# Moving four gate units and two modulation units of a streaming encoder step behind the last attention quarter and the last RWKV pair

## The chip, the cores and the metric

The kernel runs on one core of one Trainium2 chip. The metric is the device time of one execution in microseconds (us). Its engines, as the profile names them: PE (TensorE, the matmuls) with PEld (its weight loads), DVE (VectorE), ACT (ScalarE), POOL (GpSimd) and SP (SyncE, which issues nearly all DMAs). Each engine runs its own instructions in the order in which they stand in the program and waits for the others by semaphores, so the order of the rows on an engine decides what can cover a wait.

## What is computed

One layer of a hybrid encoder for 256 prompt tokens (one sequence) and 8 x 16 sample tokens, 384 tokens in all, d = 1024, in float32. The reference, cut to what matters here:

```python
mod = silu(c) @ w_ada + b_ada            # 6 rows of 1024 per sequence: shift1, scale1, gate1, shift2, scale2, gate2
h = rmsnorm(x) * (1 + scale1) + shift1
P = h @ w_in                             # columns: RWKV-7 | attention and indexer | two branch gates
o_a = rwkv7(P_rw, ...)                   # 16 heads of 64
o_b = dsa(P_dsa, ...)                    # 16 heads of 64, top-k keys by an indexer
gate_a, gate_b = split(sigmoid(P_gate + b_gate))
m = gate_a * (o_a @ w_proj_a) + gate_b * (o_b @ w_proj_b)
x = x + gate1 * (m @ w_out)
h2 = rmsnorm(x) * (1 + scale2) + shift2
x = x + gate2 * peer(h2)                 # 8 heads, 16 of 16384 experts each
```

## The kernel before

The kernel has a front (everything up to the two branch outputs), a mix (gates, projections, `w_out`) and the PEER part. The front ends at about 722 us of a span of 1794 us; the change touches the front alone.

**Units of the front.** After the head (norm, the first eight modulation units, the hidden state `LT` as a high and a low float32r part), a string `ORDER` says in which order the rest is written down, one letter a unit:

- `R`, `rwkv_pair`: two RWKV heads. Three projections of 128 columns (`shifted`), then a long chain of small steps: decay, in-chunk matrices, a triangular inverse that goes through DRAM and 15 steps on VectorE, the state chain, a group norm (`y`), and the store of the result (line 665) to `oad`. Eight pairs, 0 to 7.
- `D`, `dsa_quarter`: four attention heads. Projections K, Q, V of 256 columns each, norm and rotary, sample attention in four rounds (`attend_s`), prompt attention in two blocks (`attend_p`, which ends in `ob` and `qr`), and the store to `obd`. Four quarters, 0 to 3.
- `G`, `gate_unit`: 128 gate columns for all tokens: one weight load of 512 KB, its split into a high part (`wh`, ScalarE, line 230) and a low part (`wl`, VectorE, line 234), 24 matmuls against `LTh` and `LTl`, a sigmoid (`gg`, lines 433 and 434) and a store (line 1153). Sixteen units; nothing reads them before the mix.
- `M`, `mod_unit`: 256 columns of the modulation: two weight loads of 512 KB, eight matmuls of 32 rows against `cst` straight from the loaded weights, a copy (`mr`, line 391) and a store (line 399). Units 8 to 23 stand in `ORDER`; nothing reads them before the end of the mix.
- `I` is the indexer with its own pools, `1` to `3` choose the keys.

So G and M are fillers: they depend on the head alone and have until the mix, while R and D are chains of dependent steps.

**What sets the order.** The letters set the order in which the instructions are written down; a scheduler then places them engine by engine, earlier-written ones first where it thinks them ready. Projections of all kinds share two PSUM buffers (`mm`) and come out on PE in the order of the letters; the small steps of the pairs (`cp`, `bx`, `fx`) and quarters (`dx`) go between them.

**Weights.** All weight loads share one ring of four buffers `w` of 512 KB, four for `wh` and three for `wl` (`WB = (4, 4, 3)`). A G takes one `w` and frees it after its split; an M takes two and frees each when PE has read it. SyncE issues the loads in order.

**The end.** The mix begins with the product of `oad` and `w_proj_a`: it loads `oad` back (`px`, line 1160), splits it (`pbh`, `pbl`) and multiplies (`mm<-pbh,wh`). Its tiles lie where those of the front were.

Of the kernel before, what the change touches and what calls it, by code (L numbers as in the profile page):

```python
# [173 lines left out]

PSB = {"mm": 2, "fx": 2, "bx": 1, "dx": 2, "cp": 1}
ALIAS = {"ix": "cp", "cs": "bx", "u": "fx"}
ORDER = "GGIggggR1R23DMMMGRMRDMRGMGMRMDGMMRRMGDMMMGGGMGGM"


N1, NW, NA, NB = 36, 76, 12, 20  # L180
# [15 lines left out]
class K:  # L196
# [1388 lines left out]
    def run(self):  # L1585
        self.dense = False
        with ExitStack() as front:
# [20 lines left out]
            with ExitStack() as s:  # L1608
# [4 lines left out]
                ds, n = None, dict.fromkeys("RGD", 0) | {"M": 8}  # L1613
                for x in ORDER:
                    if x == "I":
# [130 lines left out]
```

## Time and profile before

| | |
|---|---|
| time, median of 3 runs | 1802.26 us (1799.84 to 1807.32) |
| the profiled execution | 1796.01 us |
| its span, first to last instruction | 1794.1 us |
| mean granted PE clock in it | 0.978 |
| DMA over the span | 434.11 MB, mean 242 GB/s |

A timeline row gives the start, the length, engine, line, operation, tiles (out<-in), shapes and count of merged instructions; in brackets the idle time of the engine ahead of it and what ended it. "PEclk" is the share of full clock that PE was granted. A busy PE is one with a matmul in flight, which says little about how closely they follow each other.

### The profile page before, as it was taken

The numbers are of one execution on the slowest core, as the hardware profiler recorded it, in microseconds if no ns is written. First come the engines' busy times: TensorE is split into PE (matmuls) and PEld (weight loads), VectorE is DVE, ScalarE is ACT, GpSimd is POOL, SyncE is SP. The second block draws the span as 40 slices with busy tenths as digits, with TensorE's granted clock in tenths as the row PEclk, the third lists the DMA queues.
The fourth block names the chain that finished last, engine by engine and source line by source line (L and its number), as shares of the span: only waits on it lengthen the run. The fifth ranks groups of instructions, "written<-read, shape, count | busy, mean of one in ns | idle before, by whom it ended". The sixth has DMA issues, their size and how long they took to land.

```text
span 1794.1 us, 33542 instructions
## 1 busy us (share of the span) xinstructions
PE 1714.5 (96%) x12576; PEld 1420.0 (79%) x12576; DVE 1362.0 (76%) x2945; ACT 703.2 (39%) x1411; POOL 700.5 (39%) x752
## 2 busy tenths in 40 slices
PE   6999899999999999999999989999999999999998
PEld 4987687777878877898888889999967667776656
DVE  3448777777867765445999999899958778887885
ACT  4533343333333333324222264488843333333232
POOL 2432242323423320024054446533356565555641
PEclk7999899999999999999999999999999999999999
DMA  8543652463365364665499989964579999999995
GB/s 298 161 128 96 198 178 63 155 195 97 101 198 158 85 217 151 219 202 166 151 336 333 347 305 370 376 228 164 201 267 373 364 377 379 364 395 345 376 378 182
DMA packets 181082, 434.11 MB, mean 242 GB/s; under 512 B 39348, under 2 KB 78388, under 8 KB 180920
## 3 DMA queue, kind: packets, MB, share of 16 engines
q1 hardware_dynamic: 144056, 297.73, 49.4%
q0 software_dynamic: 36864, 134.23, 20.1%
q8 instruction: 99, 1.62, 0.4%
q14 instruction: 63, 0.52, 0.1%
HBM read 401.65 MB, written 30.24 MB: 241 GB/s over the span
## 4 chain that ended last, share of the span: by engine, by line
PE 67%; DVE 15%; DMA 10%; issue 3%; ACT 2%; POOL 2%; SPq 0%; DVEq 0%; ACTq 0%; POOLq 0%
PE mm L226 24%; PE fx L226 15%; PE dx L226 12%; PE cp L226 8%; PE bx L226 7%; DVE raw L1570 2%; DMA w<-in_pv 2%; DVE wl L234 2%; DVE acc L1580 1%; DMA w<-in_w_ada 1%; DMA raw<-in_pv,pe 1%; DMA w<-in_w_in 1%; DMA w<-in_puT 1%; ACT wh L230 1%; DVE psi L1297 1%
## 5 line engine op out<-in xcount | busy, mean ns | idle before, releaser
L234 DVE TENSOR_TENSOR wl<-w,wh 128x1024 fp32r<-128x1024 f32 (+1 forms) x274 | 343.6, 1259 | 119.6 <-ACT wh L230 58.6
L230 ACT ACTIVATE wh<-w 128x1024 fp32r<-128x1024 f32 (+1 forms) x282 | 295.9, 1054 | 207.5 <-PE mm L226 83.0
L1559 POOL DMA_INDIRECT raw<-in_pu,pe x128 | 154.6, 1208 | 181.1 <-PE dx L226 56.0
L226 PE MATMUL fx<-h2h,wh 128*128 128x256 f32 x736 | 216.1, 294 | 7.5 <-ACT wh L230 4.5
L1559 POOL DMA_INDIRECT raw<-in_pv,pe x128 | 173.0, 1351 | 120.4 <-PE dx L226 44.9
L226 PE MATMUL fx<-h2h,wl 128*128 128x256 f32 x736 | 212.2, 289 | 7.7 <-DVE wl L234 7.4
L226 PE MATMUL fx<-h2l,wh 128*128 128x256 f32 x736 | 209.9, 285 | 0.0
L1580 DVE SCALAR_TENSOR_TENSOR acc<-raw,dots,acc 128x1024 f32<-128x1024 f32 x127 | 165.2, 1301 | 10.3 <-DMA raw<-in_pv,pe 9.1
L1570 DVE SCALAR_TENSOR_TENSOR raw<-raw,sh 128x1024 f32<-128x1024 f32 x128 | 161.8, 1274 | 12.5 <-DMA raw<-in_pu,pe 11.7
L226 PEld LDWEIGHTS fx<-h2h,wh 128*128 128x128 f32 x736 | 140.9, 191 | 12.3 <-ACT wh L230 5.9
L226 PEld LDWEIGHTS fx<-h2h,wl 128*128 128x128 f32 x736 | 140.2, 191 | 10.7 <-DVE wl L234 10.1
L226 PEld LDWEIGHTS fx<-h2l,wh 128*128 128x128 f32 x736 | 141.2, 192 | 2.2 <-issue 1.7
L226 PE MATMUL fx<-h2f,w 128*128 128x256 f32 x576 | 129.9, 387 | 6.0 <-ACT G L1471 3.1
L226 PEld LDWEIGHTS fx<-h2f,w 128*128 128x128 f32 x576 | 111.0, 194 | 23.2 <-ACT G L1471 4.0
L226 PE MATMUL mm<-LTh,wh 128*128 128x384 f32 (+2 forms) x352 | 125.1, 356 | 3.3 <-ACT wh L230 2.7
L226 PE MATMUL mm<-LTh,wl 128*128 128x384 f32 (+2 forms) x352 | 123.3, 350 | 0.6 <-DVE wl L234 0.6
L226 PE MATMUL mm<-LTl,wh 128*128 128x384 f32 (+2 forms) x352 | 122.8, 349 | 0.0
L226 PE MATMUL mm<-wh,LTh 128*128 128x256 f32 x336 | 97.9, 292 | 2.7 <-ACT qx L879 2.7
L226 PE MATMUL mm<-wh,LTl 128*128 128x256 f32 x336 | 97.6, 290 | 0.0
L226 PE MATMUL mm<-wl,LTh 128*128 128x256 f32 x336 | 97.3, 290 | 0.0
L1393 POOL TENSOR_TENSOR G<-G,wg 128x144 f32<-128x144 f32 (+1 forms) x64 | 55.5, 889 | 95.6 <-ACT wg L1390 95.6
L1471 ACT ACTIVATE G<-fx 128x256 f32<-128x256 f32 x76 | 28.8, 383 | 122.8 <-PE fx L226 116.6
(560 smaller groups left out, 4193.2 us busy)
## 6 DMA issues: line engine op xcount, KB each, us to landing
w<-in_puT SPq DMA_DIRECT2D x128, 512.0 KB
w<-in_pv SPq DMA_DIRECT2D x128, 512.0 KB
w<-in_w_in SPq DMA_DIRECT2D x70, 512.0 KB
w<-in_w_ada SPq DMA_DIRECT2D x48, 512.0 KB
cKT<-in_cKT SPq DMA_DIRECT2D x32, 256.0 KB
cV<-in_cV SPq DMA_DIRECT2D x32, 256.0 KB
w<-in_w_pq SPq DMA_DIRECT2D x16, 512.0 KB
d<-wst SPq DMA_DIRECT2D x8, 832.0 KB
```

The source lines that it names most:

```text
L226: return self.nc.tensor.matmul(out, l, r, start=start, stop=stop, skip_group_check=True, **kw)
L230: self.nc.scalar.activation(hi, src, AF.Copy)
L234: (self.nc.vector if eng == "v" else self.nc.gpsimd).tensor_tensor(lo, src, hi, op=OP.subtract)
L1297: nc.vector.max_index(si[:, half, h, 8:16], sv[:, half, h, 8:16], s2)
L1393: (nc.vector if w is p else nc.gpsimd).tensor_tensor(g, g, w[:, :, c0:c1], op=OP.mult)
L1471: nc.scalar.activation(g, p, AF.Gelu_apprx_tanh)
L1559: d = nc.gpsimd.indirect_dma_start(out=u, out_offset=None, in_=src, in_offset=bass.IndirectOffsetOnAxis(ap=e[:, j:j + 1], axis=0))
L1570: nc.vector.scalar_tensor_tensor(u, u, 1.0, h2, op0=OP.mult, op1=OP.mult, accum_out=dots[:, j:j + 1])
L1580: nc.vector.scalar_tensor_tensor(acc, v, dots[:, j:j + 1], acc, op0=OP.mult, op1=OP.add)
```

## The change

It is one line, the string of the front's order.

```diff
-ORDER = "GGIggggR1R23DMMMGRMRDMRGMGMRMDGMMRRMGDMMMGGGMGGM"
+ORDER = "GGIggggR1R23DMMMGRMRDMRMRMDMMRRDMMGMGMMGMGGGGGGM"
```

Up to pair 4 (`...RDMR`) the strings agree. From there, before: `GMGM R M D2 G MM R R MG D3 MMMGGGMGGM`; now: `M R M D2 MM R R D3 MMGMGMMGMGGGGGGM`. So four G and two M that stood among pairs 4 to 7 and quarters 2 and 3 stand behind the last D, and the tail behind it has nine G and seven M in place of five and five. What is computed stays the same, and the number of instructions on each engine too (SyncE's stand in three more rows). On PE the rows differ from about 350 us on, and again agree, but for a few, from the mix on.

Three places, as the built programs have them. `x8` counts equal instructions in a row; a float32 product is two records in the trace. Tile names carry the buffer's number.

The first is on PE, at the two modulation units ahead of pair 6. Before, these are the second M (`mm_6986`), small steps of pair 6 (`fx`), pair 5 (`cp`) and quarter 2 (`dx`), and then pair 6's first projection (`mm_7012`):

```order
L226 MATMUL mm_6986<-w_6987,cst 32x256 x4
L226 MATMUL mm_6986<-w_6993,cst 32x256 x4
L226 MATMUL fx_7148<-XW_416,wup_7131 128x384
L226 MATMUL fx_7152<-XW_416,wup_7131 128x384
L226 MATMUL cp_5398<-S_1072_5396,TT_5313 64x128 x8
L226 MATMUL dx_6651<-cV_6622,set_6649 32x128 x2
L226 MATMUL dx_6651<-cV_6626,set_6649 32x128 x2
L226 MATMUL dx_6651<-cV_6622,set_6649 32x128 x2
L226 MATMUL dx_6651<-cV_6626,set_6649 32x128 x2
L226 MATMUL dx_6651<-vv_6292,set_6649 32x128 x4
L226 MATMUL mm_7012<-LTh_168,wh_7004 128x384
```

Now the same two units are `mm_6849` and `mm_6865`:

```order
L226 MATMUL mm_6849<-w_6850,cst 32x256 x4
L226 MATMUL mm_6849<-w_6856,cst 32x256
L663 MATMUL bx_4341<-cfirst,y_4139 128x128 x3
L226 MATMUL mm_6849<-w_6856,cst 32x256 x3
L226 MATMUL mm_6865<-w_6866,cst 32x256
L226 MATMUL cp_5329<-TN_5316,NO_5327 64x64 x8
L226 MATMUL fx_5833<-ARp_5783,Xk_5656 64x128 x4
L623 MATMUL fx_5845<-cfirst,kk_5750 128x128 x3
L1123 MATMUL dx_6559<-cfirst,se_6555 128x128 x3
L226 MATMUL mm_6865<-w_6866,cst 32x256 x3
L226 MATMUL mm_6865<-w_6872,cst 32x256 x4
```

Behind the last of these rows stand 16 products of the inverse (`cp_5340`), six transposes of pair 5 and twelve products of quarter 2 (`dx_6565`) before pair 6's first projection (`mm_6891`). The gate unit ahead of the two is gone, and more steps of pairs 4 and 5 lie among and behind them.

The second is on PE, at the start of the tail behind quarter 3's last projection. Before, the first two of three modulation units, with steps of pair 6 and quarter 3 between:

```order
L226 MATMUL mm_8860<-w_8861,cst 32x256 x4
L226 MATMUL mm_8860<-w_8867,cst 32x256 x4
L226 MATMUL cp_7442<-Sb_7375,NX_7402 64x64 x2
L226 MATMUL bx_7482<-ARs_7178,S_1477_7479 64x32 x16
L226 MATMUL dx_8553<-cKT_8545,qTs_8213 32x256 x2
L226 MATMUL dx_8553<-cKT_8549,qTs_8213 32x256 x2
```

Now two modulation units, and a gate unit (`mm_8727`) behind them:

```order
L226 MATMUL mm_8688<-w_8695,cst 32x256 x4
L226 MATMUL mm_8704<-w_8705,cst 32x256 x4
L226 MATMUL mm_8704<-w_8711,cst 32x256
L226 MATMUL dx_8381<-cKT_8373,qTs_8041 32x256
L226 MATMUL mm_8704<-w_8711,cst 32x256 x3
L226 MATMUL cp_7269<-S_1446_7267,TT_7184 64x128 x8
L226 MATMUL dx_8381<-cKT_8373,qTs_8041 32x256
L226 MATMUL dx_8381<-cKT_8377,qTs_8041 32x256 x2
L226 MATMUL dx_8381<-kT_8044,qTs_8041 32x128 x4
L226 LDWEIGHTS expb
L226 MATMUL dx_8381<-mks_1802,expb 128x384
L226 MATMUL mm_8727<-LTh_168,wh_8722 128x384
```

The gate unit is the first of nine. The second such pair of modulation units (`mm_8806`, `mm_8822`) stands two gate units later, again with a gate unit (`mm_8845`) behind it, and 77 records between the reading of its first buffer and that unit.

The third is the last filler on PE. Before, it is followed by pair 7's state chain (`cp_7984<-cQ,bn`) and everything after it:

```order
L226 MATMUL mm_9099<-w_9100,cst 32x256 x2
L1123 MATMUL dx_8732<-cfirst,se_8728 128x128 x3
L226 MATMUL mm_9099<-w_9100,cst 32x256 x2
L226 MATMUL mm_9099<-w_9106,cst 32x256 x4
L226 MATMUL cp_7984<-cQ_7979,bn_7820 64x64 x2
```

Now the last gate unit and the last modulation unit stand ahead of pair 7's final state update (`cp_7984<-A`), and of the second block of quarter 3's prompt attention (`dx_8635<-kT`):

```order
L226 MATMUL mm_9071<-LTh_168,wl_9067 128x384
L226 MATMUL mm_9099<-w_9100,cst 32x256 x4
L226 MATMUL mm_9099<-w_9106,cst 32x256 x3
L226 MATMUL cp_7984<-A_1579_7977,bn_7699 64x128 x2
L226 MATMUL cp_7984<-ev_7980,kn_7705 64x128 x2
L226 MATMUL bx_7983<-A_1579_7977,bn_7699 64x128 x2
L226 MATMUL bx_7983<-ev_7980,kn_7705 64x128 x2
L1093 MATMUL dx_8630<-cfirst,ob_8628 128x128 x2
L226 MATMUL dx_8635<-kT_8044,qTp_8043 128x256 x2
```

The fillers reach some fifty rows further into pair 7 and quarter 3, up to the rows that began at 704 us before. Behind them the same kinds of steps are left as there, with quarter 3 somewhat ahead: both blocks' first products now come before pair 7's output is transposed.

## The prediction

> **What bounds the kernel now.** First the page: busy time by engine, the chain of work that ended last, and the group of VectorE's weight splits (busy us, mean ns of one), which is used below.
>
> ```profile
> PE 1714.5 (96%) x12576; PEld 1420.0 (79%) x12576; DVE 1362.0 (76%) x2945; ACT 703.2 (39%) x1411; POOL 700.5 (39%) x752
> ...
> PE 67%; DVE 15%; DMA 10%; issue 3%; ACT 2%; POOL 2%; SPq 0%; DVEq 0%; ACTq 0%; POOLq 0%
> ...
> L234 DVE TENSOR_TENSOR wl<-w,wh 128x1024 fp32r<-128x1024 f32 (+1 forms) x274 | 343.6, 1259 | 119.6 <-ACT wh L230 58.6
> ```
>
> TensorE (PE) is busy in 96% of the span and carries 67% of the chain, so the first question of a reordering is whether PE had idle time that another order fills. The change moves instructions only between about 350 us and the start of the mix at 722 us; behind it the order is the same but for a few rows. So next come the busy times of the stretches there (columns: busy us and instructions of each engine, the granted PE clock, DMA share, GB/s).
>
> ```profile
> core 0: us, PE busy (x) PEld busy (x) DVE busy (x) ACT busy (x) POOL busy (x), PEclk, DMA share, GB/s
> 350.00:500.00 150.00, 149.02 (x1649) 121.86 (x1650) 116.49 (x318) 51.78 (x130) 50.62 (x77) 1.00 0.46 135
> 500.00:510.00 10.00, 8.38 (x107) 5.08 (x105) 3.10 (x5) 4.48 (x9) 0.01 (x1) 1.00 0.60 179
> 510.00:520.00 10.00, 9.58 (x106) 8.73 (x107) 7.83 (x20) 5.84 (x10) 2.44 (x6) 0.83 1.04 361
> 520.00:639.00 119.00, 118.91 (x1360) 101.20 (x1359) 89.10 (x250) 38.59 (x99) 41.40 (x59) 1.00 0.39 116
> 639.00:655.00 16.00, 14.89 (x231) 9.74 (x230) 8.63 (x26) 5.65 (x15) 2.91 (x4) 1.00 0.83 260
> 655.00:694.00 39.00, 39.00 (x427) 31.64 (x417) 22.62 (x50) 16.85 (x35) 4.21 (x3) 1.00 0.74 245
> 694.00:704.00 10.00, 9.99 (x198) 8.70 (x192) 6.21 (x25) 3.01 (x14) 0.00 (x0) 1.00 0.58 196
> 704.00:722.00 18.00, 15.89 (x89) 11.65 (x87) 9.49 (x23) 4.40 (x13) 4.17 (x4) 0.65 0.26 85
> 722.00:732.00 10.00, 9.66 (x41) 8.42 (x40) 5.25 (x6) 3.91 (x6) 0.00 (x0) 0.77 1.05 373
> ```
>
> From 350 to 704 us PE stands still for 4.2 us in all (the sum of length minus busy). Three places are weak: 500 to 510, 639 to 655 and the drain from 704 to 722, where the last attention quarter and the last RWKV pair end without cover. The list of PE's waits from 480 to 780 us names the last two (total us, times, longest): at 644 us the weights of a modulation unit, in the drain VectorE's copies of the softmax.
>
> ```profile
> PE dx L226 <- DVE set L1082: 1.7, 3, 0.8
> ...
> PE mm L226 <- DMA w<-in_w_ada: 1.1, 1, 1.1
> ```
>
> **Term 1, the moved work: 0, with up to 1.3 us to gain.** What one unit costs PE is read from a gate unit that runs undisturbed, from the group of the modulation products between 639 and 694 us, and from the gate's store.
>
> ```profile
> 655.53 0.34 PE L226 MATMUL mm<-LTl,wh 128*128 128x384 f32 x1
> ...
> 658.30 0.34 PE L226 MATMUL mm<-LTh,wl 128*128 128x384 f32 x1
> ```
>
> ```profile
> L226 PE MATMUL mm<-w,cst 128*32 128x256 f32 x80 | 7.4, 387 | 1.1 <-DMA w<-in_w_ada 1.1
> ```
>
> ```profile
> L1153 SPq DMA_DIRECT2D d<-gg x16: 326/338/509, 62.0 to 694.7; - x16
> ```
>
> Sixteen steps in 2.77 us make 0.173 us a product, 24 products 4.2 us a gate unit; 80 records are five modulation units, so one takes 7.4 / 5 = 1.5 us. Four gate units and two modulation units are 4 x 4.2 + 2 x 1.5 = 19.6 us. PE is all but full where they stand, so the middle gets shorter by that, and the tail, full as well from 655 to 704, gets longer by the same: sum 0. Could they run in holes there? In the new order they reach to the rows that ran at 704 us (in the old one to 694), but the stretch 694 to 704 has only 10 - 8.70 = 1.3 us without a weight load. I take -1.0 us, with 0 and -1.3 as ends. With them move 14 issues of SyncE's queue (a load and a store for each gate unit, two loads and a store for each modulation unit), 14 x 0.34 = 4.8 us among the transfers of the last pair and quarter; DMA works 0.74 there and the queue is shown as no part of the chain, so they count nothing. POOL gets nothing to do.
>
> **Term 2, two modulation units ahead of pair 6: -3.6 us.** This is the weak place at 500 us.
>
> ```profile
> 503.17 1.93 PE L226 MATMUL mm<-w,cst 128*32 128x256 f32 x30
> 503.86 1.52 SPq L240 DMA_DIRECT2D w<-in_w_in  x2
> 508.05 1.06 ACT L230 ACTIVATE wh<-w 128x1024 fp32r<-128x1024 f32 x1 [1.49 <-DMA w<-in_w_in]
> 509.16 0.44 PE L226 MATMUL mm<-LTh,wh 128*128 128x384 f32 x1 [1.40 <-ACT wh L230]
> 510.42 0.44 PE L226 MATMUL mm<-LTh,wl 128*128 128x384 f32 x1 [0.64 <-DVE wl L234]
> 512.23 0.52 PE L226 MATMUL mm<-LTl,wh 128*128 128x384 f32 x1
> 512.55 0.52 PE L226 MATMUL mm<-LTh,wl 128*128 128x384 f32 x1
> ```
>
> Two modulation units fill all four weight buffers, and the load for pair 6 can start only when PE has read the first of them: issue at 503.86, first product at 509.16, 5.3 us. PE had 74 records to run from 503.17 to 507.76 (0.062 us each), of which some 11 were done at the issue; then it stood 1.40 + 0.64 = 2.0 us, and the clock fell: steps of 0.32 us instead of 0.173, 11 of them, 1.6 us. In the new order the same two units have 119 records of the running pairs and the quarter between the reading of the first buffer and pair 6's first product (each product in the order is two records, a transpose one); less 5 for the release, 114 x 0.062 = 7.1 us against 5.3. The wait is covered: -2.0 - 1.6 = -3.6 us, with 0 as the other end.
>
> **Term 3, the clusters in the tail: +2.6 us.** The old tail begins with three modulation units in a row (PE's 1.1 us wait above). The new one has two pairs, each with a gate unit behind it that needs the same 5.3 us. Counted as before, 52 records stand in the way at the first (3.2 us, so 2.1 us of wait) and 72 at the second (4.5 us, 0.8 us): 2.1 + 0.8 - 1.1 = +1.8 us. One of the two waits may drop the clock as at 510 us; half of 1.6 is +0.8. Ends: 0, and 1.8 + 2 x 1.6 = +5.0 us.
>
> A rule for the clock: the Trainium skill, "TensorE: Matmul & The Clock Gate", section "HAM oscillation", asks for no PE gap of more than about 3.4 us. By it neither cluster would touch the clock, and the sum would be -1.2 us instead of -2.0. The trace disagrees: gaps of 1.40 and 0.64 us came ahead of a granted clock of 0.83 in 510 to 520, so I keep the clock in.
>
> **Term 4, the drain: 0.** Its rows, from the timelines, from the last filler on:
>
> ```profile
> 692.69 1.06 PE L226 MATMUL mm<-w,cst 128*32 128x256 f32 x12
> ...
> 704.00 0.28 ACT L836 ACTIVATE y<-bx 128x128 f32<-128x128 f32 x1 [0.86 <-PE bx L226]
> ...
> 711.60 2.07 PE L226 MATMUL dx<-kT,qTp 64*128 64x256 f32 x4
> ...
> 714.01 0.85 PE L663 MATMUL bx<-cfirst,y 128*128 128x128 f32 x3
> ...
> 715.53 0.33 SPq L665 DMA_DIRECT2D d<-sq  x1
> ...
> 717.60 0.80 SPq L1160 DMA_DIRECT2D px<-d  x2
> ...
> 721.21 1.67 ACT L230 ACTIVATE pbh<-px 128x768 fp32r<-128x768 f32 x2 [4.50 <-DMA px<-d]
> ...
> 722.11 1.01 PE L226 MATMUL mm<-pbh,wh 128*128 128x384 f32 x2
> ```
>
> Pair 7's last output is copied at 704.00, normed, transposed (714.01), stored (715.53), loaded back (717.60 to 721.2) and split, and the mix starts at 722.11: 18.1 us of one thing after another. None of it changes. In the new order too, the last filler stands ahead of the rows of 704 us, so this chain runs uncovered again. Quarter 3 is ahead of where it was, so the transposes of 714.01 no longer stand behind the 2.07 us products (about -1 us), but VectorE gets a weight split (1.26 us in the mean) ahead of the rest of the group norm (about +1.3 us). I take 0; ends -2 and +2.
>
> **The sum**: -1.0 - 3.6 + 2.6 + 0 = -2.0 us. The profiled execution took 1796.0 us (span 1794.1), so 1794.0 for such an execution; it lies 6 us below the median of the three runs, 1802.3, whose spread is 1799.8 to 1807.3. Against that median the forecast is 1800 us.
>
> **Rivals.** *The drain is filled (faster).* If pair 7 and quarter 3, freed from fillers ahead of them, run early enough on the chip that PE still has gate units while they drain, the drain's holes go: 18 - 11.65 = 6.35 us without a weight load. With terms 1 and 2 at their ends and term 3 at 0: -6.35 - 1.3 - 3.6 = -11 us, 1791. For it: a clock of 0.65 there. Against it: PE takes its rows in order, and the order puts the last gate unit ahead of the drain. The Trainium skill, "Perfetto Trace Analysis", section "Identifying the Most-Contended Engine", says that weight-load time tells PE's headroom and matmul busy time doesn't; by matmul time the drain holds 2.1 us, the ten us ahead of it nothing, and this rival is -5.7 us. The trace agrees with the weight-load reading, since at half clock a busy PE is not a full one.
>
> *The middle is bound by the pairs (slower).* If without its cover an RWKV pair can't run faster, PE waits for the pairs in the middle, which then doesn't get shorter by 19.6 us, while the tail gets longer by that, less the 6.35 + 1.3 us that fit into its holes: +12 us, 1814. The stores of pairs 3 to 6 tell the pace (pair 7's stands above at 715.53):
>
> ```profile
> 487.06 0.34 SPq L665 DMA_DIRECT2D d<-sq  x1
> ...
> 552.79 0.39 SPq L665 DMA_DIRECT2D d<-sq  x1
> ...
> 612.72 0.33 SPq L665 DMA_DIRECT2D d<-sq  x1
> ...
> 668.01 0.38 SPq L665 DMA_DIRECT2D d<-sq  x1
> ```
>
> The intervals are 65.7, 59.9, 55.3 and 47.5 us, 57.1 in the mean. The new order asks for about 57.1 - 19.6 / 4 = 52 us. The rival decides if a pair can't go below 52 us; one did go at 47.5, with no successor beside it, which speaks against.
>
> *Nothing changes.* Excluded: the built order differs from about 350 us on.
>
> **How the numbers follow.** A measurement of this kernel tells about 0.5%, 9 us, from no change. Forecast (within 0.5%): 0.66. Drain filled, over 0.5% faster: 0.20. Middle bound by the pairs, over 0.5% slower: 0.14. The terms' ends give 1802 - 6.9 = 1795 and 1802 + 7 = 1809; the range goes on to the faster rival and part of the slower one, 1789 to 1811, and leaves out about 2 in 10.
>
> **What would show it.** Right: the mix starts 0 to 4 us earlier than 722 us; PE's wait at pair 6 is gone; one or two waits of 1 to 2 us on a weight load stand in the first third of the tail; the drain is again 17 to 19 us from the last copy of y to the mix, partly at half clock. Wrong: waits of PE on VectorE or ScalarE inside the pairs between 380 and 620 us (the slower rival), or a drain with gate products in it and no fall of the clock (the faster one).

## The result and the profile after

The changed kernel took 1824.70 us (median of 4 runs, 1822.95 to 1832.79) beside 1802.74 us before (median of 4, 1799.84 to 1807.32): a ratio of 1.0128, 95% interval 1.009 to 1.0166. It is slower by 22 us; the forecast was 1800.

Two quantities are used below. **Full-clock time** is the span times its mean granted PE clock: what the span would be had the clock never fallen. **Clock loss** is the rest of the span. Over the 105 executions of the kernel before that ran beside the experiments they are 1759.9 and 39.7 us in the mean (standard errors 0.4 and 0.6 us; one more execution, of 2387.71 us at a granted clock of 0.647, is left out); over 10 executions of the changed kernel (the 4 above and 6 more) 1773.8 and 48.9 (standard errors 1.0 and 1.9 us). So of some 23 us, 14 stand in the full-clock time and 9 in the clock.

The profiled execution (1826.39 us, span 1824.3) is cut at the places where it differs; the columns are those of the stretches shown of before.

```profile
340.00:357.00 17.00, 17.00 (x186) 12.91 (x186) 12.31 (x34) 4.04 (x9) 6.03 (x8) 1.00 0.75 246
357.00:369.20 12.20, 8.90 (x86) 6.08 (x85) 8.34 (x33) 2.85 (x10) 3.26 (x7) 0.86 0.48 136
...
495.00:502.30 7.30, 5.40 (x42) 4.64 (x40) 5.00 (x16) 4.25 (x7) 0.00 (x0) 0.77 0.98 349
...
598.00:625.20 27.20, 22.71 (x211) 18.95 (x209) 19.23 (x59) 5.86 (x15) 7.73 (x7) 0.81 0.28 86
...
637.00:673.00 36.00, 33.10 (x400) 25.16 (x399) 17.24 (x48) 9.25 (x20) 4.24 (x5) 0.91 0.83 275
673.00:724.00 51.00, 51.00 (x570) 43.61 (x571) 26.41 (x62) 19.27 (x42) 1.78 (x2) 1.00 0.57 175
724.00:744.00 20.00, 14.64 (x130) 10.51 (x124) 11.76 (x27) 7.18 (x19) 4.20 (x4) 0.85 0.54 171
```

PE stands still in two new stretches, 357 to 369 (3.3 us) and 598 to 625 (4.5 us), where it had been full; the weak place of before at 500 us is still there; the start of the tail is weaker (2.9 us in which PE stands still, 1.1 before); the mix starts at 744.0 instead of 722.1.

The first modulation products of the tail show where the middle ends, before and now:

```profile
639.02 1.07 PE L226 MATMUL mm<-w,cst 128*32 128x256 f32 x16
```

```profile
632.63 0.62 PE L226 MATMUL mm<-w,cst 128*32 128x256 f32 x2
```

The middle ends only 6.4 us earlier, though 19.6 us of work have left it, and from there to the mix it takes 744.00 - 632.63 = 111.4 us instead of 83.1: 28.3 more, though 19.6 have come. Both parts are worse than their share of the moved work.

PE's waits between 340 and 744 us (total, times, longest) name the new ones:

```profile
PE fx L226 <- DVE MKs L605: 7.6, 2, 4.3
PE mm L226 <- ACT wh L230: 3.0, 3, 1.5
...
PE mm L226 <- DMA w<-in_w_ada: 1.1, 1, 1.1
```

The first line has no counterpart in the kernel before. `MKs` (line 605) and `MKp` (614) are the evictions of the second of a pair's two in-chunk matrices, from the two PSUM buffers `fx`. This is how VectorE ran them at pair 3 before: the second and third of four evictions, and only then the first step of the triangular inverse (line 687), which needs `NL`, loaded back from DRAM.

```profile
357.96 0.42 DVE L605 TENSOR_TENSOR MKs<-fx,cfront 128x256 f32<-128x256 f32 x1
358.31 0.41 DVE L614 TENSOR_TENSOR MKp<-fx,cfront 128x256 f32<-128x256 f32 x1
360.67 0.15 DVE L687 TENSOR_TENSOR TX<-TL,NL 48x1 f32<-48x1 f32 x1 [1.95 <-DMA gup<-in_gup]
```

And this is what stands in the changed kernel, at pair 3 and at pair 7:

```profile
360.14 0.33 SPq L680 DMA_DIRECT2D NL<-d  x1
362.16 0.15 DVE L687 TENSOR_TENSOR TX<-TL,NL 48x1 f32<-48x1 f32 x1 [3.37 <-DMA NL<-d]
364.84 0.41 DVE L605 TENSOR_TENSOR MKs<-fx,cfront 128x256 f32<-128x256 f32 x1
365.31 0.71 PE L226 MATMUL fx<-ARp,Xk 64*64 64x128 f32 x8 [3.30 <-DVE MKs L605]
...
609.43 1.26 SPq L675 DMA_DIRECT2D d<-MBp  x2
614.23 0.33 SPq L680 DMA_DIRECT2D NL<-d  x1
616.21 0.15 DVE L687 TENSOR_TENSOR TX<-TL,NL 48x1 f32<-48x1 f32 x1 [6.48 <-issue]
618.65 0.41 DVE L605 TENSOR_TENSOR MKs<-fx,cfront 128x256 f32<-128x256 f32 x1
619.12 1.12 PE L226 MATMUL fx<-ARp,Xk 64*64 64x128 f32 x8 [4.31 <-DVE MKs L605]
```

The inverse's first step now stands ahead of three of the four evictions. VectorE takes its rows in order, idles 3.37 and 6.48 us for the round trip (store at 609.43, load at 614.23, first use at 616.21), and evicts only after four or five further steps of the inverse; until then PE can't write the next `fx`. (At pair 7 the profile names no releaser; the load had been issued 2.0 us earlier, as at pair 3.) A wait ahead of the first step was there before too (1.95 us, which the profile puts down to `gup`, another load), but only the last of the four evictions stood behind it, and PE did not wait for that one.

### The profile page after: what moved, and what is told of

Its sections match the earlier page's. It is cut to its first block, busy times and chain, and to the rows that moved or that the text cites. A ratio compares the mean times of both kernels' runs of the same rounds, so it can differ in the third digit from the quotient of the medians.

```text
span 1824.3 us, 33556 instructions
## 1 busy us (share of the span) xinstructions
PE 1721.6 (94%) x12576; PEld 1424.2 (78%) x12576; DVE 1364.1 (75%) x2945; ACT 702.1 (38%) x1411; POOL 690.4 (38%) x752
## 4 chain that ended last, share of the span: by engine, by line
PE 63%; DVE 17%; DMA 10%; issue 4%; POOL 3%; ACT 2%; SPq 0%; DVEq 0%; ACTq 0%; POOLq 0%
PE mm L226 23%; PE fx L226 14%; PE dx L226 11%; PE cp L226 7%; PE bx L226 7%; DMA raw<-in_pv,pe 3%; DVE raw L1570 2%; DVE acc L1580 2%; DVE wl L234 2%; DMA raw<-in_pu,pe 1%; DMA w<-in_pv 1%; ACT wh L230 1%; DMA w<-in_w_in 1%; DMA w<-in_w_ada 1%; DVE psi L1294 1%
## 5 line engine op out<-in xcount | busy, mean ns | idle before, releaser
L1580 DVE SCALAR_TENSOR_TENSOR acc<-raw,dots,acc 128x1024 f32<-128x1024 f32 x127 | 165.5, 1303 | 11.9 <-DMA raw<-in_pv,pe 10.7
L226 PEld LDWEIGHTS mm<-LTh,wh 128*128 128x128 f32 (+2 forms) x352 | 68.4, 194 | 10.9 <-ACT wh L230 5.8
```

Of the source, the lines that this page charges most:

```text
L226: return self.nc.tensor.matmul(out, l, r, start=start, stop=stop, skip_group_check=True, **kw)
L1580: nc.vector.scalar_tensor_tensor(acc, v, dots[:, j:j + 1], acc, op0=OP.mult, op1=OP.add)
```

## The experiments

**Theory A**: this order on VectorE is the loss. **Theory B** is the slower rival of the prediction: without fillers beside it a pair can't go faster. Later ones are C (work moved behind the last pair lengthens the front by its own length), D (the mix's first load waits for the last fillers' stores) and E (missing fillers cost clock in the middle). The table gives every run, with mean full-clock time and mean clock loss; "edge" is explained below it.

| kernel | runs | ratio to before (95%) | full clock | clock loss |
|---|---|---|---|---|
| before | 105 | 1 | 1759.9 | 39.7 |
| changed, first runs | 4 | 1.0128 (1.009 to 1.0166) | 1776.3 | 47.9 |
| changed, again | 6 | 1.0111 (1.0077 to 1.0145) | 1772.2 | 49.5 |
| changed, edge at every pair | 10 | 1.0053 (1.002 to 1.0085) | 1766.2 | 44.2 |
| before, edge at every pair | 10 | 1.005 (1.0022 to 1.0078) | 1760.2 | 48.3 |
| changed, edge at pair 7 | 4 | 1.0106 (1.0061 to 1.0151) | 1771.2 | 48.2 |
| changed, edge at 3 and 7 | 10 | 1.0086 (1.0058 to 1.0113) | 1763.1 | 51.6 |
| before, opposite edge at 3 and 7 | 10 | 1.0042 (1.0017 to 1.0067) | 1765.6 | 42.5 |
| only 4 G moved | 10 | 1.0071 (1.0047 to 1.0096) | 1769.0 | 42.0 |
| only M G ahead of the last D moved | 8 | 1.0081 (1.0055 to 1.0107) | 1764.5 | 49.2 |
| only G, G ahead of D2 and one M moved | 7 | 1.0095 (1.006 to 1.013) | 1761.8 | 56.1 |
| changed, tail without clusters | 4 | 1.0127 (1.0075 to 1.0179) | 1767.4 | 58.0 |
| before, M units apart at pair 6 | 10 | 1.0014 (0.9985 to 1.0043) | 1754.9 | 45.9 |
| changed, edge at 3 and 7, M apart | 7 | 1.0071 (1.0045 to 1.0096) | 1766.7 | 47.2 |
| before, two gates behind pair 7 | 10 | 1.0093 (1.0066 to 1.012) | 1760.1 | 54.3 |
| changed, edge at 3 and 7, pool | 4 | 1.0127 (1.008 to 1.0174) | 1766.6 | 55.6 |
| changed, pool | 4 | 1.0145 (1.0101 to 1.0189) | 1772.2 | 52.9 |
| before, M apart, pool | 10 | 0.9995 (0.9973 to 1.0017) | 1753.9 | 45.5 |
| changed, edge, one G back ahead of the last D | 10 | 1.0053 (1.0032 to 1.0074) | 1763.5 | 45.8 |
| changed, edge, one G back ahead of D2 | 10 | 1.0055 (1.0031 to 1.0079) | 1762.9 | 48.7 |

**The order on VectorE.** The edge queues each VectorE row of the inverse behind the pair's last eviction:

```diff
-                nc.vector.tensor_tensor(m_p[:, :, par], p[par], ...
+                lme = nc.vector.tensor_tensor(m_p[:, :, par], p[par], ...
...
-        TTs, TTp = self.rwkv_inverse(e, Ms[0], Mp[0])
+        with self.tc.issue_after(lme.ins):
+            TTs, TTp = self.rwkv_inverse(e, Ms[0], Mp[0])
```

In the changed kernel at every pair, and as a control in the kernel before:

> The changed kernel, with the inverse's VectorE steps of every pair queued behind the last eviction of the pair's in-chunk matrices (line 614). Theory A (in the changed order VectorE waits for the inverse's DRAM round trip, at 359 and 610 us, while evictions that PE needs stand behind it): PE's waits of 3.30 and 4.31 us at 362 and 615 us go, and with them the half clock from 365.8 to 369.2 and from 618.4 to 625.2 (1.7 + 3.4 us): 1824.7 - 12.7 = 1812 us, 1810 to 1815. Theory B (without fillers beside it a pair can't go faster, whatever VectorE's order): PE waits elsewhere in the same pairs, 1821 or more.

> The kernel before with the same edge, as a control. Theory A: no such wait of PE stands in its trace, so 1802.7 us within 3. If the edge is worth something in itself, whatever the string, it gains 6 us or more here too, 1797 or less, and the gain of the changed kernel with it would say nothing of the change. Theory B has no say.

The changed kernel fell from 1824.7 to 1812.5 us, both waits gone. The control didn't stay where it was (1811.0): its full-clock time did (1760.2), its clock loss rose by 8.6 us. So at full clock the edge is worth nothing by itself, and the gain there belongs to the changed order; but the time alone would have misled, since an edge shifts other rows and with them the clock. With the edge in both, the two kernels differ by 1.5 us in time and still by 6.0 us at full clock. Then at single pairs (`if e in (7,)`, `if e in (3, 7)`), which leaves the rows ahead untouched:

> The changed kernel with the edge at pair 7 alone: its inverse's VectorE steps queued behind the last eviction of line 614; every row of VectorE ahead of it (some 1030) as in the changed kernel. Theory A: the wait of 4.31 us at 615 us and the half clock of 618.4 to 625.2 (3.4 us) go, the one of 3.30 us at 362 us stays: 7.7 us less, 1817 us, or 1.0085 of before (1.0128 without the edge); span times clock, the time at full clock, falls by 4.3 from 1776. Theory B: PE waits elsewhere in pair 7 and nothing is gained, 1.012 or more.

> The changed kernel with the edge at pairs 3 and 7 alone. Theory A: both waits go, 12.7 us less: 1812 us, 1.0055 to 1.008 of before, and span times clock falls by 7 to 8 us. If the gain of the edge at every pair came from the other pairs, 1.0105 or more.

With both edges full-clock time is 1763.1, 10.7 us under the changed kernel's 1773.8 (7 to 8 were expected). The size is not firm: the edge at every pair gives 7.6 us, and with the pool of the fillers' results kept open in both kernels (further below) the edge at pairs 3 and 7 gives 5.6. The clock loss did not fall (51.6 us), so the time, 1.0086, stayed just above the range expected. With pair 7's edge alone full-clock time is 1771.2, only 2.6 less. In the profile with both edges (they shift line numbers by one) PE waits for no eviction of pairs 3 and 7, so theory B's "PE waits elsewhere in the same pairs" falls for these two, and pair 3 runs as before:

```profile
357.06 0.42 DVE L605 TENSOR_TENSOR MKs<-fx,cfront 128x256 f32<-128x256 f32 x1
...
359.55 0.15 DVE L688 TENSOR_TENSOR TX<-TL,NL 48x1 f32<-48x1 f32 x1
```

But the same thing now happens at pair 5, which has no edge in this kernel: VectorE stands 6.76 us for `NL`, an eviction comes behind it, and PE waits.

```profile
475.75 0.18 DVE L688 TENSOR_TENSOR TX<-TL,NL 48x1 f32<-48x1 f32 x1 [6.76 <-DMA NL<-d]
476.81 0.41 DVE L605 TENSOR_TENSOR MKs<-fx,cfront 128x256 f32<-128x256 f32 x1
477.27 1.12 PE L226 MATMUL fx<-ARp,Xk 64*64 64x128 f32 x8 [2.17 <-DVE MKs L605]
```

In all PE stands still for 8.5 us between 340 and 640 us here, for 13.8 in the changed kernel (9.9 in its second profile) and for 3.1 before.

The second runs of the changed kernel show one reason why pair 7 counts for little:

> The changed kernel unchanged, on the same chip as the run with the edge and the pool, since its four executions give its full-clock time (1776.4) and its loss to the clock (46.5) to 2 or 3 us only. All theories: 1.009 to 1.0165 of before; theory A: PE's waits of 3 to 5 us on line 605 in pairs 3 and 7 again.

Their profile has the wait at pair 3 again (3.27 us) and none at pair 7, though VectorE idles there as before:

```profile
620.27 0.36 DVE L687 TENSOR_TENSOR TX<-TL,NL 48x1 f32<-48x1 f32 x1 [3.22 <-issue]
620.36 0.65 PE L226 MATMUL fx<-ARp,Xk 64*64 64x128 f32 x8
```

```profile
605.30:619.00 13.70, 13.70 (x90) 11.20 (x87) 8.82 (x20) 3.09 (x9) 2.92 (x3) 0.50 0.44 118
```

PE had run at half clock from 605 to 619 and came late itself: the wait was paid in another coin. The opposite edge in the kernel before (three evictions queued behind the inverse's first step):

> The kernel before with the opposite edge: at pairs 3 and 7 three of the four evictions of the second in-chunk matrix are queued on VectorE behind the inverse's first step, which waits for the DRAM round trip. Theory A: PE waits 3 to 5 us on line 605 at each of the two pairs, and the clock halves behind one or both: 6 to 13 us more, 1.003 to 1.007 of before. Theory B: the order on VectorE doesn't matter, within 2 us of before.

The time came out inside theory A's range (1.0042), but not for its reason: PE waited 1.0 and 0.3 us on line 609 (605 in that file), not 3 to 5. Probably the scheduler, which knows of the edge, had placed other work in between. This run supports nothing.

**Parts of the change.** Three strings in the kernel before, from pair 4 on:

```diff
-GMGMRMDGMMRRMGDMMMGGGMGGM
+MMRMDMMRRMDMMMGMGGGGGGGGM
...
+GMGMRMDGMMRRDMMMGGMGGGMGM
...
+MRMDGMMRRMGDMMMGGMGGMGGGM
```

> The kernel before with the four gate units alone moved to the tail; the two modulation units stay among the pairs (string from pair 4 on: M M R M D M M R R M D M M M G M G and then G to the end, with the last M). 16.8 of the 19.6 us are moved, and in its built order no first step of an inverse stands ahead of more than one eviction of the in-chunk matrices at pairs 3 and 7. Theory A: no wait over 2 us of PE on line 605 between 340 and 640 us, and only clusters of the tail to pay: 1803 to 1811 us. Theory B: the pairs lose nearly all of the cover, 16.8 / 19.6 of 22 us: 1818 to 1825.

> The kernel before with one part of the change alone: the modulation and the gate unit ahead of the last D moved to the tail (5.7 of the 19.6 us). VectorE's rows agree with before down to pair 6, and no inverse stands ahead of more than one eviction of the second in-chunk matrix at pair 7. Theory A: moved work costs nothing by itself, 0 to 3 us for the tail's clusters: 0.9995 to 1.002 of before. Theory C (work moved behind the last pair stands in PE's queue ahead of that pair's steps and lengthens the front by its own length): 5.7 us, 1.003 or more.

> The kernel before with another part alone: the gate, modulation and gate units ahead of pair 5 and D2 reduced to one modulation unit (4.2 + 1.5 + 4.2 = 9.9 us moved), the rest of the middle as before. VectorE's rows at pair 3 are those of the changed kernel (three evictions behind the inverse's first step), at pair 7 those of before. Theory A: the wait of 3.3 us of PE on line 605 at about 362 us, and none at pair 7: full-clock time 3 to 5 us above before, 1.002 to 1.004. Theory C: 9.9 us, 1.005 or more.

The first moves 16.8 us of gates without the order of theory A, and still costs 9.1 us at full clock; its time, 1.0071 of before, lies between the two ranges, theory A's and theory B's. Its trace shows rows of SyncE (the pairs' stores) and PE:

```profile
607.81 0.34 SPq L665 DMA_DIRECT2D d<-sq  x1
663.41 0.33 SPq L665 DMA_DIRECT2D d<-sq  x1
718.93 0.87 PE L663 MATMUL bx<-cfirst,y 128*128 128x128 f32 x3 [3.10 <-DVE y L652]
720.42 0.32 SPq L665 DMA_DIRECT2D d<-sq  x1
727.15 1.01 PE L226 MATMUL mm<-pbh,wh 128*128 128x384 f32 x2 [7.35 <-DMA px<-d]
```

With every gate out of the middle, pairs 5 and 6 end only 4.9 and 4.6 us earlier than before (607.81 against 612.72, 663.41 against 668.01), 2 of them from ahead of the change, though 16.8 us of work are gone; pair 7 ends 4.9 later; and quarter 3 has run ahead, so that PE waits 3.10 + 7.35 us in the drain. Here theory B is right in part: the stores of pairs 3 to 7, from 485.05 to 720.42 us, come 58.8 us apart in the mean (57.1 before), so the freed time does not go to the pairs' chains. It goes to later units' projections: the tail's first modulation product runs at 620.92 us instead of 639.02. The middle of this string did get shorter by about what was moved; the loss lies behind it, where 106.2 us pass to the mix instead of 83.1. The second string costs 4.6 at full clock for 5.7 moved, as C says; its waits are again in the drain (3.5 us before the mix) and not in the middle. The third shows theory A's wait at pair 3 (3.00 us), but only 1.9 at full clock for 9.9 us moved, against C; its loss is clock, 16 us, which no theory foresaw. C as a rule falls.

**Terms 2 and 3.** The modulation units at pair 6 apart (`DMGMRR` for `DGMMRR` in the kernel before, `MRMR` for `MMRR` in the changed one with the edge), and the tail `GMGMGGMGMGGMGMGM`:

> The kernel before with the two modulation units ahead of pair 6 kept apart by the gate unit that stood in front of them (D M G M R R in place of D G M M R R). Term 2 of the prediction: the waits of 1.40 and 0.64 us at 508 us go, and with them the half clock behind: 3.6 us less, 0.998 of before. If the load for pair 6 is late for another reason (its place in SyncE's queue), the wait stays, within 1 us of before.

> The changed kernel with the edge at pairs 3 and 7, and with the two modulation units ahead of pair 6 put apart (M R M R in place of M M R R). If terms 1 and 2 add up, the full-clock time falls from 1764 with the edge alone by another 2 to 3 us, to 1761 to 1762, and the time is 1.003 to 1.006 of before. If what is left above before sits in the tail and the drain, 1764 within 2.

> The changed kernel with the same middle, but the tail's nine gate units and seven modulation units in another order, in which no two modulation units stand together (G M G M G G M G M G G M G M G M). Term 3 of the prediction: the waits of 1.50 us at 639 and of 1.13 at 669 us and the half clock behind each (1.7 us each) are the clusters', so up to 6.0 us go: 1819 to 1822 us. VectorE's order at pairs 3 and 7 is as in the changed kernel, so by theory A the waits of 3.3 and 4.3 us stay. If the tail is limited by something else (the loads themselves, or the last pair's chain between the fillers), 1824.7 within 2.

In the kernel before the waits at 508 us went, and 5.0 us of full-clock time (2.0 of waits were expected), but the clock loss rose by 6.2 and the time stayed (1.0014). In the changed kernel with the edge nothing was gained. The tail without clusters lost its waits at 639 and 669 us and 6.4 us of full-clock time, had both of theory A's waits (3.0 and 5.1 us), and lost 9 us more to the clock; its time, 1.0127, is that of the changed kernel.

**The drain.** In the kernel before, the last two gates queued on PE behind the product that ends pair 7's output:

> The kernel before with its last two gate units queued on PE behind the product that ends pair 7's output (2 x 4.2 us of work out of the last pair's way and into the drain; the tail's order is M M M G G G M M G G). If the end of the front is set by pair 7's chain, which stands behind the fillers in PE's queue, that chain comes 6 to 8 us earlier and the gates fill the drain (2.2 us of waits and 6.3 us lost to the clock there): 4 to 8 us less, 0.9955 to 0.998 of before. If PE's work sets the end, or the gates' splits delay the group norm, within 2 us.

It took 1815.95 us, a clear miss: pair 7's store came at 728 us instead of 715.5, later and not earlier, and the clock loss rose by 14.6. Then the pool of the fillers' results kept open to the end of the mix (`self.fill` opened in `front` in place of `fh`):

> The changed kernel with the edge at pairs 3 and 7, and with the pool of the fillers' results (mr, gg) kept open to the end of the mix, so that the mix's first load px doesn't lie over them and doesn't wait for the last filler's store (3.7 us of SyncE on the store of mr in the run with the edge alone; px was issued 8.0 us behind pair 7's store instead of 2.1 as in before). Theory D (the rest of the loss sits in the drain, at this wait): px 2 to 3 us behind pair 7's store, PE's wait of 8.8 us at 728 us down to 3 or 4, full-clock time from 1764 to about 1759, time 1.005 to 1.007 of before instead of 1.0086. If the rest sits in the middle or is the clock's, full-clock time 1764 within 2.

> The changed kernel with the fillers' pool alone kept open. Theory D: its px waited 3.1 us behind pair 7's store where before waits 2.1, so no more than 1 to 2 us: 1.010 to 1.013 of before; the two waits on VectorE in pairs 3 and 7 stay.

> The kernel before with the modulation units ahead of pair 6 apart and the fillers' pool kept open: as a candidate that beats both. The first took 3.3 us off the full-clock time and nothing off the time; the second should take nothing here (px waits for pair 7's store itself). 0.998 to 1.002 of before.

Theory D fell. In the first of these the mix's load no longer waits for `mr`, and is as late:

```profile
724.66 1.87 SPq L240 DMA_DIRECT2D w<-in_w_proj_a  x3
726.58 0.43 SPq L666 DMA_DIRECT2D d<-sq  x1
...
734.73 0.80 SPq L1161 DMA_DIRECT2D px<-d  x2
```

```profile
SPq L1161 <- DMA d<-sq: 3.9, 1, 3.9
```

Pair 7's store was issued behind three weight loads of 512 KB, and the mix's load waited for it until 734.7; the `mr` wait had only been the last of several. That the loads make the store late is likely, but no run moved them. The pool changed nothing in the two others either; the last is no faster than before (0.9995), though 6.0 us better at full clock.

**The clock.** One gate unit put back from the tail, at either of two places of the middle near which the clock had halved (`MMRRGD`, and `MGDMM`), with the edge at pairs 3 and 7:

> The changed kernel with the edge at pairs 3 and 7, and one gate unit put back from the tail to where one of the four had been, ahead of the last D. Theory E (in the changed order the middle has stretches of small products alone, and behind these the clock halves without any wait, as at 601 to 605 us for 10 us in several profiles): the half clock near 600 us shrinks to 3.4 us or none, the loss to the clock falls from 52 (with the edge alone) to 45 to 48, time 1.005 to 1.007 of before. If it is not the fillers that keep the clock, the loss stays at 50 to 56 and the time at 1.0086 or more; if moved work costs its own length (theory C) the full-clock time falls by 4 as well.

> The same, but the one gate unit put back ahead of D2 (behind the modulation unit of pair 5), some 100 us earlier. Theory E: the half clock at 453 to 477 us goes rather than that near 600, loss to the clock 45 to 48, 1.005 to 1.007 of before. Otherwise as with the other place: 50 to 56, 1.0086 or more.

At the first place time and clock loss came out where theory E has them. The stretch behind 600 us with the edge alone, and then two stretches with the gate unit:

```profile
603.50:613.70 10.20, 10.20 (x86) 8.88 (x85) 5.41 (x9) 0.66 (x2) 0.31 (x1) 0.50 0.48 140
```

```profile
600.00:613.00 13.00, 13.00 (x142) 10.70 (x142) 11.26 (x21) 2.69 (x8) 7.83 (x7) 1.00 0.43 137
...
455.00:475.50 20.50, 20.50 (x137) 16.30 (x137) 14.12 (x29) 2.60 (x7) 6.17 (x8) 0.51 0.21 61
```

Clock loss fell from 51.6 to 45.8 us, full-clock time stayed, and the ratio went from 1.0086 to 1.0053 (the two intervals overlap). At the second place the half clock between 453 and 484 us shrank from 13.7 us to 3.4 while that near 608 stayed (10.2 us); 48.7 us lost, a little more than expected. So in one profile each, a filler brought the clock back at its own place. It did not bring it back for the middle as a whole: with the gate unit at the first place the clock halved for 20.5 us behind 455, where the edge alone has 13.7 us in three pieces, and between 300 and 640 us the profiles lose 13.7 us with the edge alone and 11.9 with either gate unit. Nor is it shown that density did it: with the edge alone each of these half-clock stretches begins behind a wait of PE (0.97, 1.37 and 2.17 us; 1.76 on the group norm, line 653, ahead of 603), and the last one went too. The amount of filler is not the rule: the string that moves all four gates loses 42.0, the one that moves two gates and a modulation unit 56.1. It may count which small steps and waits stand together; no run separates that.

## Why the prediction was wrong

- **Term 1, -1.0, is the step that failed.** "The middle gets shorter by that", and the tail longer by the same, took it that moving fillers leaves the other rows as they are. (The unit costs as printed make 19.8 us, unrounded 19.6.) The middle ended 6.4 us earlier instead of 19.6, or 9.8 counted from pair 0's store, and the rest up to the mix grew by 28.3. The prediction looked at the new order on PE alone; VectorE's order had changed too, at pair 3 already. Two waits of 7.6 us in all came into the middle, and edges that take them out take 5.6 to 10.7 us off the 14 of full-clock time. Between 300 and 640 us the profiles lose 10.2 us to the clock (15.4 in the second one) where 1.7 was lost; 1.7 of that, behind 318 us, stands ahead of the first changed row. The edges do not make term 1 right: with them at pairs 3 and 7 the tail starts at 631.80 us in the profile, still only 7.2 earlier. And with four gates moved the middle was right and the tail was not.
- **Term 2, -3.6, failed**; the wait is there again:

```profile
487.92 1.05 PE L226 MATMUL mm<-w,cst 128*32 128x256 f32 x10
488.82 0.33 SPq L680 DMA_DIRECT2D NL<-d  x1
490.67 0.89 SPq L240 DMA_DIRECT2D w<-in_w_in  x2
497.29 0.44 PE L226 MATMUL mm<-LTh,wh 128*128 128x384 f32 x1 [1.26 <-ACT wh L230]
498.55 0.44 PE L226 MATMUL mm<-LTh,wl 128*128 128x384 f32 x1 [0.64 <-DVE wl L234]
```

  The cover was counted rightly (PE ran 8.1 us from the first reading), but 5.3 us was taken as the price from the release on. SyncE had four loads of pair 5 and quarter 2 ahead of this one, so it was issued 2.75 us behind the first reading, and from there to the product took 6.6 us.
- **Term 3, +2.6, had the waits right and the clock wrong**:

```profile
640.47 0.45 PE L226 MATMUL mm<-LTh,wh 128*128 128x384 f32 x1 [1.50 <-ACT wh L230]
...
667.63 0.44 PE L226 MATMUL mm<-LTh,wh 128*128 128x384 f32 x1 [0.27 <-ACT wh L230]
...
669.95 1.08 PE L226 MATMUL mm<-w,cst 128*32 128x256 f32 x8 [1.13 <-DMA w<-in_w_ada]
```

  1.50 + 0.27 + 1.13 - 1.11 = 1.8 us of waits, as worked out; the clock halved for one slot behind both (1.7 us each), where +0.8 stood for half a chance of one: +5.2 in all, just over the upper end of 5.0.
- **Term 4, 0, was right**:

```profile
725.71 0.28 ACT L836 ACTIVATE y<-bx 128x128 f32<-128x128 f32 x1 [0.86 <-PE bx L226]
...
736.57 0.32 SPq L665 DMA_DIRECT2D d<-sq  x1
739.67 0.80 SPq L1160 DMA_DIRECT2D px<-d  x2
...
744.00 1.01 PE L226 MATMUL mm<-pbh,wh 128*128 128x384 f32 x2 [2.55 <-ACT pbh L230]
```

  744.00 - 725.71 = 18.3 us, beside 18.1. The load follows the store by 3.1 us instead of 2.1, quarter 3 ends ahead of the mix instead of inside it, and PE waits 2.55 us where it had run, but for less time at half clock (10.2 us instead of 17.1).
- **The rivals.** The faster one did not happen. The slower one had the right sign and nearly the right sign-post (waits of PE on VectorE inside the pairs between 380 and 620 us; they came at 362 and 615), at a chance of 0.14 and a price of +12, which even so is only about half of the loss. Its premise, that a pair does not get faster without cover, holds in the string with four gates moved, without any wait of theory A; its consequence does not: there the middle got shorter, PE stood still for 6.8 us between 340 and 640 us (3.1 before), and 10.5 us of waits came in the drain instead.
- **What stays open.** With the edge at pairs 3 and 7, some 3 us at full clock and 12 us of clock are left over before. The first would fit the tail's 1.8 us of waits and pair 5's 2.2, but no run took them out in that kernel one by one. The second moves with every edit; one gate unit at one place took off 5.8 us, with the reservations above. So the cause is shown for a part of the full-clock time, and open for the clock. In the profile, 3.4 of the 21.9 us by which the mix is late are there before the first changed row (pair 0's store at 300.5 instead of 297.1): the clock was low for 13.7 instead of 6.8 us from 202 us on. The change does not make that: the kernel before with two gates behind pair 7, whose string is the same up to there, has 13.7 us too.

## What to carry to other kernels

When a scheduler places the rows, compare the order on every in-order engine, not only on the one that looks full: a row that waits for a DRAM round trip is harmless until an eviction that PE needs stands behind it. Fillers taken out of the chains' neighbourhood did not speed the chains up here; they let later units run ahead, so look at what then covers the end. And split a small difference into full-clock time and clock loss before giving it a cause: here several edits lowered the one and raised the other.

## What the runs showed of the hardware

The granted clock moves in slots of 3.413 us on a fixed grid: in each of the 20 profiles all half-clock stretches behind 100 us start on one. The slot before decides most of it. Over the 20 profiles, from 300 us on, all of 104 slots at full clock in which PE was busy under 40% were followed by a half one; of 244 with 40 to 65%, 85; of 8121 with more, 25. In between the same gap can go either way. A wait of 1.58 us stands in both kernels' profiles and ends at 313.63 us before and at 317.03 in the changed one; it left its slot 56% busy before, and the clock stayed, and 54% in the changed kernel, and the clock halved. With the edge at pairs 3 and 7 it lay across two slots (66 and 88% busy), and the clock stayed. Two places of the changed kernel:

```profile
597.90:601.30 3.40, 3.40 (x42) 2.28 (x40) 2.89 (x7) 0.37 (x2) 1.82 (x2) 1.00 0.30 116
601.30:604.70 3.40, 3.22 (x17) 2.85 (x13) 3.03 (x9) 0.97 (x3) 0.59 (x1) 0.50 0.36 117
...
614.95:618.36 3.41, 0.00 (x0) 0.00 (x0) 1.84 (x11) 0.00 (x0) 0.00 (x0) 1.00 0.22 43
618.36:625.20 6.84, 6.08 (x32) 5.75 (x32) 6.50 (x24) 0.88 (x2) 2.27 (x1) 0.50 0.08 29
```

The lower pair is the wait at pair 7: an empty slot, then two at half clock. The upper pair has no wait at all: PE is busy for all of the slot, but mostly with products that use half of the 128 x 128 array or less (64 x 128, 64 x 64, 32 x 64). Each product's columns can be weighted by the share of the array that it uses and added up in the slot in which it starts. Then, from 300 to 760 us, none of 1688 slots at full clock with 3250 or more columns was followed by half clock, 34 of 693 between 1500 and 3250, and 57 of 81 below; but most of the 81 are slots with gaps. Of slots in which PE was busy over 95%, 3 of 12 below 1500 columns and 7 of 561 between were followed by half clock, and none of 1592 above. So a stretch of small products alone can lose the clock, but it seldom did. The Trainium skill, "TensorE: Matmul & The Clock Gate", section "Part 1: The HAM clock gate", describes such a free-running window of 3413 ns, and the grid agrees; its section "HAM oscillation" puts the limit at gaps of more than 3.4 us, and here a gap of 1.58 us did the same, and a few slots without a gap.
